# First three loads of a row-gradient kernel issued from Pool's queue, one packet per DMA engine

## The chip, the core and the metric

The kernel runs on one core of one Trainium2 chip. The metric is the device time in microseconds (us) of that core for one execution; lower is better. A core has engines that compute (here VectorE, called DVE, and GpSimd, called POOL), an engine that here only issues transfers (SyncE, called SP), and 16 DMA engines that move data between the chip's memory (DRAM) and the on-chip memory. The on-chip memory has 128 partitions. An engine that issues a transfer does not wait for it; whoever needs the data waits on a semaphore which the transfer raises when it has landed.

## The reference

```python
def setup_inputs():
    return {"x": np.random.randn(8192, 8192).astype(np.float32)}

def reference(x):
    return np.gradient(x, axis=1)
```

For each row this is half the difference of the right and the left neighbour, and in the first and the last column the plain difference of the two outermost elements. The input and the output are 268.4 MB each, and each element is read once and written once.

## The kernel before

The 8192 rows are cut into 32 sets of 256 rows. A set is one tile of 128 partitions with two whole rows in each (16,384 floats, 64 KB per partition), so a load or a store of a set is one transfer of 8.39 MB. Three buffers (`slots`, `NB = 3`) take the sets in turn: set i lies in slot i % 3. A slot is 64 floats longer than the two rows; a load writes from float 64 on, the result is written from float 0 on, over the input, and the store sends floats 0 to 16,383.

For each set i the kernel records:

- a load (`load(i)`, L50 to L53), issued on SP's queue, which for i of 3 or more waits until the store of set i - 3 has landed, since that frees the slot;
- a small POOL subtraction (L74) which takes the four end differences of the two rows into `ends`, after the load has landed;
- the one large DVE operation (L80), half the difference of neighbours over the whole tile, after the subtraction;
- a small copy (L91) that puts the four end values into the result, on DVE or, for 12 of the sets, on POOL;
- a store (`store`, L55 to L64), issued on SP's queue after the copy.

The order of the work on each queue is the order in which it is written (`manual_schedule`). SP's queue begins with loads 0, 1 and 2 (L68 and L69), then stores 0, 1, 2, loads 3, 4, 5, stores 3, 4, 5 and so on. A store of the middle set of a group of three (i % 3 == 1) is held back: it is recorded after the next set's subtraction, and it waits for that subtraction, so for the next load to have landed (`held`, L93 to L97). SP works through its queue in order: an instruction that waits holds up all that stand behind it. On POOL's queue, four small fills of constants stand first, then the subtractions and copies in order of the sets.

Below, "load 2" or "store 0" mean the transfer of that set; L with a number, as in L74, is a line of the kernel.

Of the kernel before, what the change touches and what calls it, by code (L numbers as in the profile page):

```python
# [1 line left out]

# [4 lines left out]


@with_exitstack
def kernel(  # L10
    ctx: ExitStack,
    tc: tile.TileContext,
    x: bass.AP,
    out: bass.AP,
):

    nc = tc.nc
    P = nc.NUM_PARTITIONS
    n, m = x.shape
    R = 2  # L20
    NB = 3
    SH = 64
    W = R * m
    nsets = n // (P * R)
    f32 = x.dtype

    x_sets = x.rearrange("(s p t) m -> s p (t m)", p=P, t=R)
    out_sets = out.rearrange("(s p t) m -> s p (t m)", p=P, t=R)

    pool = ctx.enter_context(tc.tile_pool(name="pool", bufs=1))  # L30
    edge = 256 // 4
    nends = nsets * R * 2
    ends_pad = pool.tile([P, nends + edge // 2], f32, name="ends", tag="ends")
    ends = ends_pad[:, 0:nends].rearrange("p (s t e) -> p s t e", t=R, e=2)
    slots = [pool.tile([P, SH + W], f32, name=f"slot{k}", tag=f"slot{k}") for k in range(NB)]
    loads, stores = [], [None] * nsets
    in_front = {}

    def chain(i, ins, *needed):

        group, engine = f"slot{i % NB}", ins.ins.engine
        keep = [o.ins for o in needed]
        if in_front.get(engine, (None,))[0] == group:
            keep.append(in_front[engine][1])
        tc.declare_no_dep(ins.ins, group=group, keep=keep, reason="implied by the needed step")
        tc.add_to_no_dep_group(group, ins.ins)
        in_front[engine] = group, ins.ins
        return ins

    def load(i):  # L50
        b = slots[i % NB]
        ins = nc.sync.dma_start(out=b[:, SH : SH + W], in_=x_sets[i])  # L52
        loads.append(chain(i, ins, *([stores[i - NB]] if i >= NB else [])))  # L53

    def store(i, done, later):  # L55
        ins = nc.sync.dma_start(out=out_sets[i], in_=slots[i % NB][:, 0:W])
        stores[i] = chain(i, ins, done)
        if later is not None:
            tc.add_manual_dep(
                ins.ins,  # L60
                later.ins.name,
                mybir.DependencyInfo(mybir.DependencyClass.Sync, mybir.DependencyReason.DATA),
                reason="issued once the next tile has landed",
            )  # L64

    held = None
    with tc.manual_schedule():
        for i in range(NB):  # L68
            load(i)  # L69
        for i in range(nsets):  # L70
            b = slots[i % NB]
            xin = b[:, SH : SH + W].rearrange("p (t m) -> p t m", m=m)

            ins = nc.gpsimd.tensor_sub(  # L74
                out=ends[:, i, :, :],
                in0=xin[:, :, 1 : m : m - 2],
                in1=xin[:, :, 0 : m - 1 : m - 2],
            )
            at = [chain(i, ins, loads[i])]
            ins = nc.vector._custom_dve(  # L80
                dve_ops.TENSOR_TENSOR_REDUCE_SUB_MAX,
                out=b[:, 1 : W - 1],
                in0=b[:, SH + 2 : SH + W],
                in1=b[:, SH : SH + W - 2],
                s0=0.0,
                s1=0.5,
            )
            halved = chain(i, ins, *at)
            res = b[:, 0:W].rearrange("p (t m) -> p t m", m=m)
            placer = nc.gpsimd if i % 5 in (1, 3) and i < nsets - 2 else nc.vector  # L90
            ins = placer.tensor_copy(out=res[:, :, 0 : m : m - 1], in_=ends[:, i, :, :])  # L91
            placed = chain(i, ins, halved)
            if held is not None:  # L93
                store(*held, at[0])
                held = None
            if i % NB == 1 and i + 1 < nsets:
                held = i, placed  # L97
            else:
                store(i, placed, None)
            if i % NB == NB - 1:  # L100
                for k in range(i + 1, min(i + 1 + NB, nsets)):
                    load(k)


# [1 line left out]
_INS = ['x']  # L106
_OUTS = [((8192, 8192), 'float32')]


# [23 lines left out]
```

## Time and profile before

| what | value |
|---|---|
| median of 3 runs | 1246.8 us (1246.67 to 1247.39) |
| the profiled execution's own time | 1246.62 us |
| its span, first to last instruction | 1244.7 us |
| DVE busy | 554.6 us, 45% of the span |
| POOL busy | 8.8 us, 1% of the span |
| DMA: packets, bytes, mean rate | 9217, 536.88 MB, 431 GB/s |
| one large DVE operation (L80) | 17,224 ns, 32 of them |
| one end subtraction on POOL (L74) | 198 ns, 32 of them |

The span is what the profile covers; 1.9 us of the execution's own time lie outside of it. Busy time is time in which an engine works on an instruction; the issuing of transfers is not counted as busy. The DMA share of a stretch of time counts each packet where it starts, so that in stretches shorter than a packet it swings between 0 and several; rates in such stretches are read as "so many packets began here".

### The profile page before, as it was taken

The page shows a single profiled execution, that of the slowest core. Times are in us where ns is not written, and L with a number is a line of the kernel's source. Part 1 is how long each engine was busy: PE and PEld are TensorE (multiplying, and loading weights), DVE is VectorE, ACT ScalarE, POOL GpSimd, SP SyncE. Part 2 cuts the span into 40 slices and gives each one's busy share as a digit, 9 for nine tenths or more (in the row PEclk, how much of TensorE's full clock was granted, in tenths as well). Part 3 has the DMA queues.
Part 4 walks back from the last instruction along what each step waited for, and adds up shares of the span by engine and source line. Part 5 has one row for each costly group of instructions (what it writes and reads, how often), then busy time and mean ns, then how long its engine had stood idle before and what let it go on. Part 6 is the DMA issues. An engine that isn't in the chain of part 4 may idle for free.

```text
span 1244.7 us, 237 instructions
## 1 busy us (share of the span) xinstructions
DVE 554.6 (45%) x52; POOL 8.8 (1%) x48
## 2 busy tenths in 40 slices
DVE  2850582079009702850582079009603840591082
POOL 0000000000000000000000000000000000000000
DMA  9999999999999999999999999999999999999999
GB/s 404 438 436 423 421 438 438 438 438 428 432 430 430 438 438 438 423 436 436 430 434 436 438 428 432 438 436 434 425 436 434 432 436 436 436 434 430 434 409 404
DMA packets 9217, 536.88 MB, mean 431 GB/s; under 512 B 1024, under 2 KB 1024, under 8 KB 1024
## 3 DMA queue, kind: packets, MB, share of 16 engines
q1 hardware_dynamic: 9216, 536.88, 99.8%
q14 instruction: 1, 0.01, 0.0%
HBM read 268.44 MB, written 268.44 MB: 431 GB/s over the span
## 4 chain that ended last, share of the span: by engine, by line
another core or an unknown queue 74%; DVE 18%; DMA 3%; issue 2%; POOL 1%; SPq 0%; POOLq 0%
DVE slot L80 18%; DMA slot<-in_x_dram 3%; POOL ends L74 0%; POOL slot L91 0%; SPq L52 0%; POOLq L128 0%; DVE slot L91 0%
## 5 line engine op out<-in xcount | busy, mean ns | idle before, releaser
L80 DVE CUSTOM_DVE_ANT_0 slot<-slot 128x16382 f32<-128x16382 f32 x32 | 551.2, 17224 | 667.6 <-POOL ends L74 667.6
L74 POOL TENSOR_TENSOR ends<-slot 128x4 f32<-128x4 f32 x32 | 6.3, 198 | 988.5 <-DMA slot<-in_x_dram 988.5
L91 POOL COPY slot<-ends 128x4 f32<-128x4 f32 x12 | 2.3, 190 | 207.9 <-DVE slot L80 207.9
L91 DVE COPY slot<-ends 128x4 f32<-128x4 f32 x20 | 3.4, 172 | 0.7
L117 POOL MEMSET const-bfloat16-1.0<- 128x1 bf16 x1 | 0.1, 101 | 0.0
L117 POOL MEMSET const-uint8-127<- 128x1 uint8 x1 | 0.1, 101 | 0.0
L117 POOL MEMSET const-float32-0.0<- 128x1 f32 x1 | 0.1, 98 | 0.2 <-issue 0.2
L117 POOL MEMSET const-float32-1.0<- 128x1 f32 x1 | 0.1, 98 | 0.0
## 6 DMA issues: line engine op xcount, KB each, us to landing
slot<-in_x_dram SPq DMA_DIRECT2D x32, 57.9
out_dram<-slot SPq DMA_DIRECT2D x32, 40.2
```

The source lines that it names most:

```text
L74: ins = nc.gpsimd.tensor_sub(out=ends[:, i, :, :], in0=xin[:, :, 1 : m : m - 2], in1=xin[:, :, 0 : m - 1 : m - 2],)
L80: ins = nc.vector._custom_dve(dve_ops.TENSOR_TENSOR_REDUCE_SUB_MAX, out=b[:, 1 : W - 1], in0=b[:, SH + 2 : SH + W], in1=b[:, SH : SH + W - 2],
L91: ins = placer.tensor_copy(out=res[:, :, 0 : m : m - 1], in_=ends[:, i, :, :])
L117: nc = _bacc.Bacc("TRN2", target_bir_lowering=False, num_devices=1)
```

## The change

The first three loads, those of sets 0, 1 and 2, are issued on POOL's queue in place of SP's, and each is marked as a single packet: the part of the transfer that one of the 16 DMA engines carries forms one packet. The other 29 loads and all 32 stores stay on SP's queue as they were.

```diff
     def load(i):
         b = slots[i % NB]
-        ins = nc.sync.dma_start(out=b[:, SH : SH + W], in_=x_sets[i])
+        if i < NB:
+            ins = nc.gpsimd.dma_start(out=b[:, SH : SH + W], in_=x_sets[i], single_packet=True)
+        else:
+            ins = nc.sync.dma_start(out=b[:, SH : SH + W], in_=x_sets[i])
         loads.append(chain(i, ins, *([stores[i - NB]] if i >= NB else [])))
```

In the built program POOL's queue then holds, after its four fills and the barrier at the start, the three loads, and behind them the first subtraction. SP's queue begins with store 0, which waits for the copy of set 0. What each instruction waits for is otherwise the same step as before; the semaphores have other numbers. Nothing of the computation changes.

## The prediction

> **What bounds the kernel now.** I read the page first: the shares of busy time and the rows of DMA.
>
> ```profile
> DVE 554.6 (45%) x52; POOL 8.8 (1%) x48
> ...
> DMA  9999999999999999999999999999999999999999
> ...
> DMA packets 9217, 536.88 MB, mean 431 GB/s; under 512 B 1024, under 2 KB 1024, under 8 KB 1024
> ...
> q1 hardware_dynamic: 9216, 536.88, 99.8%
> ```
>
> The reader is to see that the 16 DMA engines are busy for 99.8% of the span and no compute engine for half of it. There are 64 transfers of 8.39 MB; 9216 packets are 64 x 16 x 9, so each engine carries eight pieces of 65.5 KB of every transfer and a small closing packet (1024 of them). A piece takes 0.998 x 1244.7 x 16 / 8192 = 2.43 us, a transfer 8 x 2.43 = 19.4 us. The end is therefore set by when the engines start, by what 512 pieces each take, and by any time an engine stands without a piece.
>
> Second, the timeline of the start, which gives the order around the first three loads:
>
> ```profile
> 0.74 1.32 SPq L52 DMA_DIRECT2D slot<-in_x_dram  x3
> 22.69 0.20 POOL L74 TENSOR_TENSOR ends<-slot 128x4 f32<-128x4 f32 x1 [22.25 <-DMA slot<-in_x_dram]
> 22.93 17.23 DVE L80 CUSTOM_DVE_ANT_0 slot<-slot 128x16382 f32<-128x16382 f32 x1 [22.93 <-POOL ends L74]
> 40.19 0.17 DVE L91 COPY slot<-ends 128x4 f32<-128x4 f32 x1
> 40.38 40.01 SPq L56 DMA_DIRECT2D out_dram<-slot  x3
> 41.99 0.20 POOL L74 TENSOR_TENSOR ends<-slot 128x4 f32<-128x4 f32 x1 [19.10 <-DMA slot<-in_x_dram]
> ...
> 62.37 0.20 POOL L74 TENSOR_TENSOR ends<-slot 128x4 f32<-128x4 f32 x1 [2.67 <-DMA slot<-in_x_dram]
> ```
>
> SP issues the three loads within 1.32 us; they land at about 22.7, 42.0 and 62.4, one transfer apart. Store 0 is issued at 40.38, while load 1 is still moving, and waits on the same queue behind load 2.
>
> Third, busy time by stretches. A packet is counted where it begins, so GB/s times length over 65.5 KB is the number of pieces that begin:
>
> ```profile
> 1.50:2.00 0.50, 0.00 (x0) 0.00 (x0) 1.00 4.20 1442
> 2.00:2.50 0.50, 0.00 (x0) 0.00 (x0) 1.00 1.43 524
> 2.50:3.00 0.50, 0.00 (x0) 0.00 (x0) 1.00 0.30 131
> 40.38:40.90 0.52, 0.00 (x0) 0.00 (x0) 1.00 0.00 0
> 40.90:41.25 0.35, 0.00 (x0) 0.00 (x0) 1.00 4.35 1873
> 41.25:41.70 0.45, 0.00 (x0) 0.00 (x0) 1.00 2.03 874
> ...
> 1204.00:1204.40 0.40, 0.00 (x0) 0.00 (x0) 1.00 0.00 0
> 1204.40:1204.60 0.20, 0.00 (x0) 0.00 (x0) 1.00 11.49 4915
> ```
>
> At the start 11 engines begin in 1.5 to 2.0 us, 4 by 2.5 and the last by 3.0: 0.8 to 2.2 us after SP's issue at 0.74. Load 2 begins on 10 engines in 40.90 to 41.25 and on 6 in 41.25 to 41.70. Near the end the engines have run dry and store 30, issued at 1203.60 by the timeline, begins on 15 of them in 1204.40 to 1204.60: 0.8 to 1.0 us after the issue.
>
> **The change, part by part.** *Removed:* three issues on SP, 1.32 us. SP next has store 0 at 40.38, so nothing that sets the end gains from this.
>
> *Added on POOL:* three issues ahead of the first subtraction (L74). POOL is idle for 22.25 us there, so the subtraction is late only if issuing takes longer than a load; without that cover, whatever the issuing took would pass to DVE. What is on the path is the time until POOL's first load reaches all engines, since every engine then works without a break and hands a late start on to the end: the one stretch where engines run dry, before 1204.40, lies behind the landing of load 30, which is late by as much. POOL can begin at about 0.7 us, as SP does after the same barrier. Its price for an issue is not in this trace. Low bound: it is as quick as SP at 1203.60, all engines starting within 1.0 us; then the last engine starts at 1.7 in place of some 2.75, a gain of 1.1 us. Middle: one small POOL step for each of the 16 engines, at 0.098 us (the shortest POOL row, a fill) to 0.198 us (the subtraction), 1.6 to 3.2 us, then the 0.9 us from handing over to the first piece: 0.7 + 1.6 + 0.9 = 3.2 to 0.7 + 3.2 + 0.9 = 4.8, which is 0.45 to 2.05 us later than 2.75. High bound: a step of 0.098 us for each of the 128 partition rows, 12.5 us, 11.4 us later. I take the middle of the middle case, +1.25 us, because 16 shares are what both the old and the new queue hand out; -1.1 and +11.4 stay as ends.
>
> By the Trainium skill, DMA: Bandwidth & Descriptors, Specifications, the first byte comes about 1 µs after an issue from GpSimd and about 0.6 µs after one from SP; an estimate from that page would be +0.4 us here. The row above has 0.8 to 2.2 us for SP, so the measurement is longer than the page's figure for SP, and no run so far shows POOL's.
>
> *One packet per engine.* The same bytes move in the same pieces or in one run of eight. Were the seams between pieces all that goes, the gain is what 24 pieces lose to them; the mean piece of 2.43 us over everything leaves no room for more than about 1% of it, 24 x 0.02 = 0.5 us. In the other direction the three loads are 58 us of DMA time, and each per cent that they run slower costs 0.58 us. I take nothing, with -0.5 and +6 (ten per cent) as bounds.
>
> *Moved between queues.* Load 2 and store 0 no longer stand in one queue. If load 2 still goes first the order of everything is the old one. SP's later work is untouched: it issues store 1 after load 2's subtraction, and the engines still hold store 0 (19.4 us) then. Three more landings that SP checks at its end are long over; at 17 ns for such a wait (SP's shortest row on L56) that is 0.05 us.
>
> Sum, against the profiled execution: 1246.62 + 1.25 + 0.05 = 1247.9 us (span 1244.7 + 1.3 = 1246.0). The median of the runs lies 0.18 us above that execution, so the forecast is 1248.1 us.
>
> **The rivals.** *Store 0 overtakes load 2.* Store 0 can start 0.85 to 1.0 us after its issue, so at 41.23 to 41.38; 6 of the 16 engines take up load 2 only in 41.25 to 41.70, and all of this shifts together with the start. In one queue the order was given; in two, the engine that finds both waiting may take the store. If it takes one piece, load 2 lands 2.4 us later, which the 19.4 us of store 0 still cover: no cost. If it takes all eight pieces, load 2 lands 19.4 us later even with one such engine, at about 81.8. Then store 1, which is held for that landing, finds empty engines: about 0.4 us from the last piece to the subtraction (41.70 at most to 41.99 is 0.3), 0.23 for it (22.69 to 22.93), 0.9 to the first piece, so 1.5 us in which nothing moves. With the late start that makes 1246.8 + 1.3 + 1.5 = 1249.6 us. For it speaks the tie in time; against it, that 10 engines start load 2 before store 0 can be there, and the marking as one packet, if the engine has already taken up that packet. The Trainium skill, DMA: Bandwidth & Descriptors, Queues, rings and completion order, says that an engine takes turns between queues packet by packet; by that rule this overtaking can happen at the seam after load 1 and load 2 is then not interrupted. No row of this trace has two queues at work.
>
> *POOL's issue is much dearer, or its loads run slower.* It decides from where issuing passes some 3.5 us, or the loads' rate falls by 5%. With 5 to 11.4 us: 1252 to 1258 us. Against it: POOL's rows here are all below 0.2 us, and the mean piece is the same for loads and stores as far as the trace separates them.
>
> *POOL's queue starts sooner.* All engines begin within 0.2 us of each other, as store 30 does: -1.1 us, and at most another -0.5 for seams, 1245.2 to 1245.7 us. For it speaks the spread of over 1 us between the engines at the start; against it, that this spread may belong to a cold first read and not to SP's queue.
>
> *The marking has no effect* and the engines alternate between load 2 and store 0: both end near 81, the same hole of 1.5 us, the same 1249.6 us. It is held within the first rival.
>
> **How the numbers follow.** What a measurement of this kernel can tell from no change is about 0.2%, 2.5 us, so the borders are 1244.3 and 1249.3. The forecast (start later by 0.2 to 2.5 us, old order) has 0.42, its own range 1247.0 to 1249.3; overtaking or alternating 0.28; the dear issue or slower loads 0.17; the sooner start 0.13. Overtaking lies above the border in about three of four cases (0.21), the dear issue always (0.17), the forecast now and then (0.04): slower 0.42. Faster needs 2.5 us where the rows give at most 1.6; of the sooner start's 0.13 I leave 0.08 for a gain that they do not show. The rest, 0.50, is within. The range takes in the sooner start and the overtaking with a later start than I took: 1245.4 to 1252.5, leaving out most of the dear issue and part of the gain.
>
> **What would show each step.** First pieces of POOL's load between 3.2 and 4.8 us in the stretches, the first subtraction near 24.0 and not 22.69. Load 2 landing one transfer after load 1, with store 0 behind it: order kept. Load 2's subtraction near 82 and a hole in the DMA row there: overtaken. Loads landing more than 19.6 us apart: the packet is slower. A first subtraction before 22.7 makes my start price wrong in sign; one past 27 makes it wrong in size.

## The result, and the profile after

The changed kernel takes 1249.34 us in the median of 18 runs (1248.01 to 1258.11), the kernel before 1246.76 us beside it (18 runs, 1245.78 to 1247.71). By the medians it is slower by 2.6 us, 0.2%. The ratio of the means is 1.0027 (95% interval 1.0015 to 1.0038); two executions of 1257 and 1258 us draw it up. The profiled execution took 1249.09 us with a span of 1247.2 us, 2.5 us over the span before.

The page shows who moves what. Queue 0 is POOL's, queue 1 SP's; then comes the row of POOL's three issues:

```profile
q1 hardware_dynamic: 8784, 511.71, 94.8%
q0 software_dynamic: 432, 25.17, 4.8%
...
L53 POOL DMA_DIRECT2D slot<-in_x_dram x3 | 1.7, 587 | 0.8 <-PEq L131 0.8
```

432 packets are 3 transfers x 16 engines x 9: a load marked as a single packet is still recorded as eight pieces and a closing packet on each engine, so that a marked part forms one packet, as the change has it, is not seen in this trace. An issue holds POOL for 0.59 us; SP's median is 0.34 us.

The timeline of the start:

```profile
1.25 1.75 POOL L53 DMA_DIRECT2D slot<-in_x_dram  x3 [0.80 <-PEq L131]
23.50 0.19 POOL L77 TENSOR_TENSOR ends<-slot 128x4 f32<-128x4 f32 x1 [20.50 <-DMA slot<-in_x_dram]
...
41.18 57.33 SPq L59 DMA_DIRECT2D out_dram<-slot  x3
42.79 0.20 POOL L77 TENSOR_TENSOR ends<-slot 128x4 f32<-128x4 f32 x1 [19.10 <-DMA slot<-in_x_dram]
...
80.49 0.20 POOL L77 TENSOR_TENSOR ends<-slot 128x4 f32<-128x4 f32 x1 [19.99 <-DMA slot<-in_x_dram]
...
98.55 23.52 SPq L55 DMA_DIRECT2D slot<-in_x_dram  x3
```

POOL issues from 1.25 us, 0.5 us after SP did. Loads 0 and 1 land 0.8 us later than before, load 2 lands 18.1 us later, at 80.5. SP's three stores now spread over 57 us and not 40, because store 1 is held until load 2 has landed. Its issue, before and after:

```profile
62.60 0.34 SPq L56 DMA_DIRECT2D out_dram<-slot  x1
80.71 0.34 SPq L59 DMA_DIRECT2D out_dram<-slot  x1
```

Busy time by stretches, read as before (GB/s x length / 65.5 KB = pieces that begin), gives the first pieces:

```profile
2.50:3.00 0.50, 0.00 (x0) 0.49 (x1) 1.00 3.91 1311
3.00:3.50 0.50, 0.00 (x0) 0.00 (x0) 1.00 1.68 655
3.50:4.00 0.50, 0.00 (x0) 0.00 (x0) 1.00 0.31 131
```

10, 5 and 1 engines begin here, 1.25 to 2.75 us after POOL's issue; it was 0.8 to 2.2 us after SP's. By the Trainium skill, DMA: Bandwidth & Descriptors, Specifications, the first byte would come some 1 µs after a GpSimd issue and 0.6 µs after one from SP; both are longer here; the order agrees, and the difference of 0.45 to 0.55 us is near the page's 0.4.

After store 0's issue, the DMA view of the changed kernel has one queue alone in each of three stretches of 0.8 us. The rows belong to 47.8 to 48.6, 50.2 to 51.0 and 52.6 to 53.4 us:

```profile
q1 hardware_dynamic: 16, 1.05, 302.2%
...
q0 software_dynamic: 16, 1.05, 302.2%
...
q1 hardware_dynamic: 16, 1.05, 302.2%
```

On all 16 engines a piece of store 0, then one of load 2, then one of store 0: the engines take turns, piece by piece, until both are through near 81.

A hole is a stretch in which an engine stands without a piece. The last view goes after time that is lost without one, in pieces that take longer than the others. The stretches hold 16 beginning pieces each, so the DMA share times the length is the mean time of one piece. First the kernel before, then the changed one, at the last piece of store 2 and of load 5:

```profile
116.90:117.60 0.70, 0.00 (x0) 0.00 (x0) 1.00 3.45 1498
174.90:175.60 0.70, 0.70 (x1) 0.00 (x0) 1.00 3.50 1498
```

```profile
117.90:118.75 0.85, 0.00 (x0) 0.00 (x0) 1.00 3.43 1234
176.40:177.80 1.40, 1.40 (x1) 0.00 (x0) 1.00 2.49 749
```

Before, 3.45 x 0.70 = 2.42 and 2.45 us; after, 3.43 x 0.85 = 2.92 and 2.49 x 1.40 = 3.49 us. In the mean an engine loses 0.5 us at the one place and 1.0 at the other, some more than others. Such pieces are not new: in the kernel before, the last pieces of load 2, where the engines go over from loads to stores for the first time, take 6.13 x 0.55 = 3.37 us.

```profile
58.10:58.65 0.55, 0.55 (x1) 0.00 (x0) 1.00 6.13 1907
```

Near 81, where the prediction had put a hole, there is none:

```profile
79.00:81.50 2.50, 0.78 (x1) 0.20 (x1) 1.00 0.97 419
81.50:82.50 1.00, 1.00 (x1) 0.00 (x0) 1.00 2.43 1049
```

In 79.0 to 81.5 some 16 pieces begin, the last of store 0; in the next 1.0 us the first 16 of store 1, one piece later on every engine. So the view after gives 0.8 us at the start and 1.5 us in long pieces near 118 and 177, against 2.5 us of span in all; what the rest of the trace holds stands further below. The experiments had to say what brings the long pieces.

### The profile page after: what moved, and what is told of

Read it like the earlier page. It is cut to its first block, busy times and chain, and to the rows that moved or that the text cites. A ratio compares the mean times of both kernels' runs of the same rounds, so it can differ in the third digit from the quotient of the medians.

```text
span 1247.2 us, 236 instructions
## 1 busy us (share of the span) xinstructions
DVE 554.6 (44%) x52; POOL 10.6 (1%) x51
## 4 chain that ended last, share of the span: by engine, by line
another core or an unknown queue 69%; DVE 19%; DMA 7%; issue 2%; POOL 1%; SPq 0%; POOLq 0%; PEldq 0%
DVE slot L83 19%; DMA slot<-in_x_dram 7%; POOL ends L77 0%; POOL slot L94 0%; POOL slot L53 0%; DVE slot L94 0%; SPq L59 0%; POOLq L131 0%; PEldq L131 0%
```

## The experiments

Each kernel was timed beside the kernel before on the same chip, whose median was 1246.9 to 1247.3 us there. Differences are of medians; in brackets stands the 95% interval of the ratio of means, turned into us. Theory A, with which I began, put the rest of the loss on the taking of turns.

**1. Without the mark.**

```diff
-nc.gpsimd.dma_start(out=b[:, SH : SH + W], in_=x_sets[i], single_packet=True)
+nc.gpsimd.dma_start(out=b[:, SH : SH + W], in_=x_sets[i])
```

> The changed kernel without the single-packet mark. Theory A (0.8 us of the loss is POOL's later start; the other 1.7 us come from load 2 and store 0 sharing the engines piece by piece, which the mark does not prevent): the same trace, first subtraction near 23.5, load 2's subtraction near 80.5, time 1249.3 +-0.5 us. Rival M (the mark did hold a part of the transfer together, since two pieces of load 2 went ahead of store 0's first): without it store 0 comes in one piece earlier and the time moves by more than 0.5 us. Rival B (POOL's queue as such costs the 2.5 us, the exchange nothing): 1249.3 as well; this run does not tell A from B.

Measured: 1249.22 us, +1.9 (1.1 to 4.1). First subtraction at 23.82, load 2's at 80.99. This trace too has 432 packets on POOL's queue. The mark does nothing that the time or the trace shows; rival M falls.

**2. The first three loads on ScalarE's queue.**

```diff
-nc.gpsimd.dma_start(out=b[:, SH : SH + W], in_=x_sets[i], single_packet=True)
+nc.scalar.dma_start(out=b[:, SH : SH + W], in_=x_sets[i])
```

> The first three loads on ScalarE's queue, without mark: two queues as in the changed kernel, but POOL issues nothing. Theory A: first subtraction near 22.7 as in the kernel before, load 2's subtraction near 80, time 1246.8 + 1.7 = 1248.5 us. Rival B: the time of the kernel before, 1246.8 +-0.4 us, although load 2 lands near 80.

Measured: 1248.02 us, +0.7 (-0.3 to 1.9), first subtraction at 22.52, load 2's at 79.33. The start's cost is gone with POOL's issue. What is left is smaller than theory A had it, and the interval doesn't part it from nothing. Store 1 is issued at 79.55, and the long pieces are there, 3.49 x 0.80 = 2.79 and 5.15 x 0.65 = 3.35 us:

```profile
116.80:117.60 0.80, 0.00 (x0) 0.00 (x0) 1.00 3.49 1311
175.30:175.95 0.65, 0.65 (x1) 0.00 (x0) 1.00 5.15 1613
```

**3. Store 0 behind load 2 on POOL's queue.**

```diff
-        ins = nc.sync.dma_start(out=out_sets[i], in_=slots[i % NB][:, 0:W])
+        queue = nc.gpsimd if i == 0 else nc.sync
+        ins = queue.dma_start(out=out_sets[i], in_=slots[i % NB][:, 0:W])
```

> The changed kernel with store 0 on POOL's queue too, behind load 2 in the same queue. Theory A: first subtraction near 23.5, load 2's subtraction back at 42.8 + 20.4 = 63.2, only the start is lost, 1246.8 + 0.8 = 1247.6 us (stores 0 and 1 now share the engines, which costs nothing if only reads against writes do). Rival B: 1249.3 us, since POOL's queue is used as much and more.

Measured: 1248.66 us, +1.4 (0.3 to 2.4), first subtraction at 23.49, load 2's at 63.59. One queue for both restores the order, as expected, and some of the loss is gone. What is left is 0.6 us more than the start's 0.8; 0.3 of it stands behind the last piece, as is shown below, and the rest lies inside the interval.

**4. Everything on POOL's queue.** Loads (marked) and stores alike.

```diff
-        if i < NB:
+        if True:
             ins = nc.gpsimd.dma_start(out=b[:, SH : SH + W], in_=x_sets[i], single_packet=True)
...
-        ins = nc.sync.dma_start(out=out_sets[i], in_=slots[i % NB][:, 0:W])
+        ins = nc.gpsimd.dma_start(out=out_sets[i], in_=slots[i % NB][:, 0:W])
```

> All 32 loads (marked) and 32 stores on POOL's queue: one queue again, no exchange anywhere. Theory A: the start's 0.8 us and up to 0.5 us more where store 30 is issued into empty engines, 1247.6 to 1248.1 us. Rival B: the cost grows with POOL's share, well over 1250 us.

Measured: 1259.01 us, +11.7 (10.6 to 13.8). The page of this run:

```profile
q0 software_dynamic: 9216, 536.88, 99.4%
```

A piece takes 0.994 x 1256.6 x 16 / 8192 = 2.44 us in the mean, 0.013 more than before, 6.9 us over 512 pieces; the engines stand empty for 0.6% of the span and not 0.2%, another 5 us, of which 2.6 lie between the last piece and the end. Theory A's number is wrong here: POOL's queue costs more than its start when it is used throughout. The longer mean is not spread over all pieces: the median piece takes 2.418 us in both traces, and the last pieces of eight transfers, between 351 and 528 us and again between 936 and 1114, take 3.2 to 3.4. Why was not followed up. What three loads on POOL's queue cost without a late store 1 is measured in experiments 3 and 7.

**5. One queue, store 0 ahead of load 2.** On SP's queue of the kernel before.

```diff
-        for i in range(NB):
+        for i in range(NB - 1):
             load(i)
...
                 store(i, placed, None)
+            if i == 0:
+                load(NB - 1)
```

> The kernel before with one step moved: on SP's queue store 0 stands ahead of load 2, so load 2 lands near 81 and stores 1 and 2 are issued as late as in the changed kernel, but in one queue, with no two transfers taking turns. What the trace of the changed kernel loses at 116 us (0.6 us per engine) and at 174 us (1.1 us) is the question. Theory T (taking turns between two queues brings it): no long pieces at 116 and 174 us; a hole of about 1.2 us near 81, since store 1 is issued only when load 2 has landed and nothing else is left, so about 1.2 us over the kernel before. Rival S (the late load 2 and the later issue order bring it): long pieces at both places, 1.2 + 0.7 = 1.9 us over the kernel before.

Measured: 1251.65 us, +4.4 (2.6 to 5.7). Its timeline:

```profile
82.11 0.20 POOL L74 TENSOR_TENSOR ends<-slot 128x4 f32<-128x4 f32 x1 [22.56 <-DMA slot<-in_x_dram]
82.33 17.81 SPq L56 DMA_DIRECT2D out_dram<-slot  x2
```

Store 1 comes at 82.33, the engines stand empty from about 81 to 83 (no piece begins in 79.5 to 83.0), and the long pieces are there at both places, though no two queues take turns in this kernel. Its stretches, 16 pieces each:

```profile
119.40:119.70 0.30, 0.00 (x0) 0.00 (x0) 1.00 10.34 3495
178.00:178.60 0.60, 0.60 (x1) 0.00 (x0) 1.00 5.82 1748
```

10.34 x 0.30 = 3.10 and 5.82 x 0.60 = 3.49 us. Theory T, that turns bring them, falls. The loss is more than twice what either theory had: the hole near 81 takes 2.1 us in the mean of the engines, not 1.2, and the long pieces come on top. Left are the late load 2 or the late store 1.

**6. All loads on ScalarE's queue.**

```diff
-        ins = nc.sync.dma_start(out=b[:, SH : SH + W], in_=x_sets[i])
+        ins = nc.scalar.dma_start(out=b[:, SH : SH + W], in_=x_sets[i])
```

> All 32 loads on ScalarE's queue, all stores on SP's: loads and stores take turns in every group, the suspected cost many times over. Theory T: clearly slower, more than 3 us over the kernel before. Rival N (taking turns costs nothing beyond the first group, what was seen is a matter of how the start falls): within 1 us of the run with the first three loads there, 0.7 us over the kernel before.

Measured: 1274.84 us, +27.5 (25.3 to 28.8). It looks like a win for theory T and is not one: with loads no longer behind stores, load 3 lands 13 us earlier and load 5 21 us later than before, so the issue of every store moves too. The run shows that reads on one queue and writes on another cost 2.2% in this kernel, not which part of that is the turns. Its store 1 is issued late too, at 79.52, but with other transfers around it, so it speaks neither for nor against what follows.

**7. Store 1 not held, in the changed kernel.**

```diff
-                store(*held, at[0])
+                store(*held, at[0] if i > NB else None)
```

> The changed kernel, with store 1 no longer held until load 2 has landed. In the trace of the changed kernel store 1 is issued 0.2 us after load 2's landing at 80.5 and its first piece follows store 0's last without a gap at 81.7. Theory T: nothing was lost there, so nothing is won, 2.0 to 2.6 us over the kernel before, long pieces at 116 and 174 us again. Rival H (as the prediction had it, the held store 1 leaves a hole): 1.5 us faster than the changed kernel.

Measured: 1248.36 us, +1.1 (0.5 to 2.6), some 1.5 us less than the changed kernel's 2.5 (experiment 11). The two intervals overlap, so the times alone do not settle it. Store 1 is issued at 60.73; the turns are still taken and load 2 still lands at 80.4. There was no hole to win (theory T's point), and yet time is won (rival H's number, not its reason): load 3 lands 1.1 us later than in the kernel before, where it was 2.2 us in the changed kernel, and the pieces at the two places take 1.21 x 2.00 = 2.42 and 1.34 x 2.00 = 2.68 us:

```profile
117.00:119.00 2.00, 0.00 (x0) 0.00 (x0) 1.00 1.21 524
175.00:177.00 2.00, 2.00 (x1) 0.00 (x0) 1.00 1.34 524
```

This points at store 1's issue.

**8. The end: load 30 ahead of store 29, in the kernel before.**

```diff
+                if i == nsets - NB:
+                    load(i + 1)
                 store(i, placed, None)
...
-                    load(k)
+                    if k > len(loads) - 1:
+                        load(k)
```

> The kernel before, with load 30 issued ahead of store 29 on SP's queue. A test of the step that any time in which the engines stand empty is handed on to the end: in the kernel before they run dry before 1204.40 us, 0.6 to 2.5 us by engine, 1.1 us in the mean. With load 30 a transfer earlier store 30 is ready before load 31 has moved, and there is no such hole. Theory T: 1 us faster than the kernel before, 0.6 to 1.5. Rival: same time, the engines lose it at another place.

Measured: 1247.34 us, +0.0 (-0.9 to 1.4). Load 30 lands 18.9 us earlier and store 30 is issued at 1184.71, but load 31 lands where it did (its subtraction is at 1205.60, before at 1205.22), and store 31 waits for that, one DVE operation and a copy: the engines now run dry between stores 30 and 31 instead. A hole in front of a chain that waits for something else is worth nothing.

**9. ScalarE's queue and store 1 not held.** Experiments 2 and 7 together.

```diff
-nc.gpsimd.dma_start(out=b[:, SH : SH + W], in_=x_sets[i], single_packet=True)
+nc.scalar.dma_start(out=b[:, SH : SH + W], in_=x_sets[i])
...
-                store(*held, at[0])
+                store(*held, at[0] if i > NB else None)
```

> The first three loads on ScalarE's queue and store 1 no longer held: load 2 and store 0 still take turns, POOL issues nothing, store 1 is issued near 59.6. Theory L (of the loss, POOL's later start is one part, and the other is store 1's issue moved from 62.6 to 80.7 us, behind load 2's late landing, while the taking of turns itself costs nothing): no long pieces at 116, at most 0.3 us per engine at 174, and the time of the kernel before within 0.4 us. Rival T (the turns cost): 0.7 us over it, as with the first three loads there and store 1 held.

Measured: 1246.71 us against 1246.94, -0.2 (-1.5 to 0.8). Load 2's subtraction is at 79.13, so turns are taken as in the changed kernel. At the same two places:

```profile
116.70:117.40 0.70, 0.00 (x0) 0.00 (x0) 1.00 3.45 1498
174.70:175.40 0.70, 0.70 (x1) 0.00 (x0) 1.00 3.63 1498
```

Pieces take 2.42 and 2.54 us. Store 1 is issued at 59.71. Turns between two queues, and a load that lands 17 us late, cost nothing by themselves that this interval (up to 0.8 us) shows.

**10. Only store 1 late, in the kernel before.**

```diff
-                store(*held, at[0])
+                store(*held, at[0] if i > NB else placed)
```

> The kernel before with one wait changed: store 1 waits for the copy of set 2, so it is issued near 80.1 and not at 62.6, while store 0 is still moving until 80.8. One queue, no turns, load 2 early, POOL issues nothing. Theory L: long pieces at 116 and 174 us as in the changed kernel (0.5 and 1.0 us per engine), 0.7 to 1.3 us over the kernel before, of which up to 0.3 is a short hole near 81. Rival (load 2's late landing, not store 1's, brings them): no long pieces at 116, at most 0.3 us over the kernel before.

Measured: 1248.80 us, +1.9 (0.8 to 2.9). Store 1's issue, and the stretches of this run:

```profile
80.19 0.34 SPq L56 DMA_DIRECT2D out_dram<-slot  x1
...
81.00:81.50 0.50, 0.00 (x0) 0.00 (x0) 1.00 4.93 2097
...
117.30:117.70 0.40, 0.00 (x0) 0.00 (x0) 1.00 7.76 2621
175.90:176.50 0.60, 0.60 (x1) 0.00 (x0) 1.00 5.54 1748
```

All 16 engines begin store 1 in 81.0 to 81.5, with next to no hole behind store 0. The pieces take 7.76 x 0.40 = 3.10 and 5.54 x 0.60 = 3.32 us. One queue, load 2 early (its subtraction at 62.44), POOL issuing nothing: a late issue of store 1 alone brings both groups of long pieces and a loss of their size. Experiment 2 has the same issue and the same long pieces and lost 0.7 us, so the price in time is known only as somewhere from 0.7 to 1.9.

**11. The changed kernel again.** No edit.

> The changed kernel again, beside the two others on one chip, for a second trace. Theory L: first subtraction 0.8 to 1.0 us later than in the kernel before, long pieces at 116 and 174 us again, 2.0 to 2.6 us over the kernel before. Rival (the long pieces were chance in one execution): none at these places.

Measured: 1249.47 us, +2.5 (1.5 to 3.7). First subtraction at 23.70; load 3 lands 2.7 us later than in the kernel before, as in the first trace (2.2), and load 5 4.5 us later (4.0).

```profile
117.90:118.90 1.00, 0.00 (x0) 0.00 (x0) 1.00 2.92 983
176.00:178.50 2.50, 2.50 (x1) 0.00 (x0) 1.00 1.38 419
```

With 15 and 16 beginning pieces that is 2.92 x 1.00 x 16 / 15 = 3.1 and 1.38 x 2.50 = 3.45 us. The long pieces are no accident of one execution.

**12. No store held, in the kernel before.**

```diff
-                store(*held, at[0])
+                store(*held, None)
```

> The kernel before with no store held: each middle store is issued as soon as its copy is done, some 2 to 3 us earlier in every group (store 1 at 59.7 and not at 62.6, store 4 near 176.5 and not at 178.6). The kernel before loses some 1.3 us per engine to long pieces near 290, 522, 638 and 869 us. Theory L carried further (a middle store issued earlier means fewer long pieces, in every group): up to 1.3 us faster than the kernel before. Rival (only an issue close to the moment the engines run out of work does it, and 18 us of work in hand are as good as 21): the time of the kernel before within 0.4 us.

Measured: 1246.92 us against 1247.27, -0.4 (-1.5 to 0.8). The time is the rival's: 18 us of work in hand are as good as 21, as far as an interval that reaches 1.5 us of gain can say. The trace speaks for the rival too, as it has long pieces near 408, 640 and elsewhere with every store issued early. None of the versions is shown to beat the kernel before.

## Why the prediction came out as it did

**The bound** was read rightly: the DMA engines are still busy for 99.6% of the span (99.8% before), and what is lost early reaches the end in part. Of load 5's 4.0 us, 2.3 are left when load 30 lands.

**The start** had the right sign and nearly the right size. I took 1.25 us from a range of 0.45 to 2.05; the traces have 0.8 us, 1.0 in experiments 7 and 11, 1.1 in 1, 0.7 in 4. It came out by other parts than I took: 10 of the 16 first pieces begin before 3.0 us, where one POOL step for each engine would have had them in 3.2 to 4.8. Of the loss, 0.5 us is there because POOL's first issue comes at 1.25 and not at 0.74, the rest lies between issue and first piece. Experiments 2, 9 and 10, where POOL issues nothing, have the old start.

**The end** was mis-sized: the sum has 0.05 us for it. The packets' own times put the end of the last piece 1.16 us before the end of the span in the kernel before (1.16 to 1.18 in all runs where POOL issues nothing), and 1.43 in the changed one (1.43 to 1.50 in experiments 1, 3, 7 and 11). So POOL's issuing costs 0.3 us more at the end; what takes the time there is open. Start and end together make 1.0 to 1.4 us, and experiments 3 and 7, where store 1 is issued early, lost 1.4 and 1.1.

**The order was not kept.** The forecast's own condition, that load 2 goes first and SP's work is untouched, is the step that failed. What came is what the prediction had as "the marking has no effect", held within the first rival: the engines alternate. Store 0 did not take all of its pieces first either; two of load 2's pieces were through on every engine, and from 47.9 us on the turns were one piece each. The Trainium skill, DMA: Bandwidth & Descriptors, Queues, rings and completion order, says that an engine takes turns packet by packet. The trace agrees if a piece of 65.5 KB counts as a packet. The page gives a packet as typically 9 to 17 descriptors; if a recorded piece is one descriptor, the trace differs from that, marked or not, since experiment 1 has the same trace without the mark.

**The price of that rival, 1.5 us, was about right in size and wrong in kind, so the agreement is luck.** I had priced a hole of 1.5 us near 81, between load 2's landing and store 1's first piece. I had forgotten that an engine that takes turns ends with a piece of the other transfer: after load 2's last piece comes store 0's, 2.4 us, and this covers the subtraction, SP's issue at 80.71 and the 0.9 us to the first piece. The time went elsewhere: with store 1 issued near 80 and not at 62.6, an engine loses in the mean 0.5 us at the end of store 2 and 1.0 at the end of load 5. Experiment 10 shows it with nothing else changed, experiments 7 and 9 show it all but go when store 1 is issued early, experiment 5 shows it without two queues. By the packets' own times, pieces beyond 2.418 us cost an engine 1.4 to 1.9 us between 110 and 185 us in the six traces with store 1 issued near 80 (the changed kernel, experiments 1, 2, 5, 10 and 11), and 0.1 to 0.4 in the seven with it issued near 60 (experiment 6 left aside). So the chain is: own queue for load 2, turns with store 0, load 2 late by 18 us, store 1 held for it, long pieces. The sum of its two ends, 1.1 us (experiment 7) and 1.9 us (experiment 10), is 3.0 against 2.5 to 2.6 measured, within the intervals; with the 0.7 of experiment 2 in place of the 1.9 it is 1.8. Why a store that arrives just in time makes pieces 35 and 95 us later longer is open. The sum of the forecast had one piece time for all pieces, the mean of 2.43 us. Its own rows spoke against that: load 2's subtraction came 20.4 us after load 1's, not 19.3, because of the long pieces near 58.

**The whole trace.** Divided over the profiled pair, the 2.5 us of span are, in the mean of the engines: empty 1.0 us longer at the start, 0.7 longer ahead of store 30 and 0.3 longer behind the last piece; long pieces 1.6 us more between 110 and 185 us and 1.0 less after that. Past 185 us the runs scatter (experiments 4 and 6 left aside): an engine loses 0.6 to 2.3 us there with store 1 late and 1.3 to 2.1 with it early. Whether some of an early loss is made up there, or the profiled pair differs by chance, is open. The wider hole ahead of store 30 comes from engines that have drifted apart: store 30 waits until load 30 has landed on the slowest of them, and that one finished 2.4 us behind the mean of the 16, not 1.8.

**The size:** +1.3 us was forecast, +2.6 measured, the time within the range. The median lies a few hundredths of a us above the border at 1249.3, between the two cases that had most of the chance, so which side of the border it fell on says nothing. The forecast's own case, with the order kept, is nearest to experiment 3, and there its +1.3 stands against 1.4 measured.

**The dear issue and the slower loads** did not come: a piece of load 2 takes what all others take (3.022 x 0.80 = 2.42 us in 50.2 to 51.0). The sooner start did not come either.

## What to carry to other kernels

When transfers are split over two queues, look for the wait that relied on one queue's order: the turns showed no cost here, the store that was held for the load did. A second queue that is slower to its first piece (here 0.7 to 1.1 us) is paid for where the DMA engines are full from start to end, and so is its end (0.3 us). A time lost without a hole is found by the mean length of a piece, stretch by stretch, and not by looking for idle engines. Do that over the whole trace: a loss found at one place can be made up at another.

## What was not expected of the hardware

A late issue is paid long after: 0.5 and 1.0 us per engine at 118 and 177 us for a store issued at 80, with next to no hole behind it. Putting everything on POOL's queue cost 11.7 us, and loads on one queue with stores on another 27.5 us, although the bytes and the engines are the same. And 2 of the 18 executions of the changed kernel took 1257 and 1258 us, as did 1 of 12 without the mark (1258.4), while none of the kernel before did; no trace shows what happened in them.
